# Row normalisation by the sum of magnitudes: eleven tiles of 12 and 8 rows against ten contiguous tiles of 13 and 12 rows

## The chip, the core and the metric

The kernel runs on one core of a Trainium2 chip. The metric is the time of one execution on the device, in microseconds; lower is better. The time before is the median of three runs.

## The reference

Each row of 1024 numbers is divided by the sum of its magnitudes.

```python
x = np.random.randn(32, 512, 1024).astype(np.float32)

def reference(x):
    sums = np.sum(np.abs(x), axis=-1, keepdims=True)
    return (x / (sums + 1e-8)).astype(np.float32)
```

Flattened, these are 16,384 rows of 4,096 bytes: 67.11 MB are read and 67.11 MB are written.

## The kernel before

The 16,384 rows are dealt to the 128 partitions of the on-chip memory, 128 rows to each. Work goes tile by tile; a tile holds so many rows in every partition. There are eleven tiles, numbered 0 to 10: ten of 12 rows and a last one of 8.

Where the rows lie in memory: the first 32 rows of every partition form a block called the head, in which a partition's rows are 32 x 4,096 = 131,072 bytes apart from the next partition's. Tiles 0 and 1 take rows 0 to 23 of the head, and tile 10 takes the last 8 rows of it. Tiles 2 to 9 are each one contiguous stretch of memory, in which partitions are 12 x 4,096 = 49,152 bytes apart.

Four buffers of 12 rows go round. `load(i)` (its transfer is issued at L86, on the queue of SyncE, SP) fills one; `store(i)` (issued at L91, on the queue of ScalarE, ACT) empties it; `load(i + 4)` can be issued only when the store of tile i has landed. The order is written out by hand: four loads, and then for each tile the computation, the store and the load of the tile four places on.

`max_dma_last_dim` sets the longest contiguous piece, here called a packet, that one descriptor of a transfer moves. A partition's share of a 12-row tile is 49,152 bytes; it goes as one packet (`WHOLE`) or as two of 24,576 (`HALF`). Loads of tiles 0 and 1 and stores of tiles 9 and 10 are whole; the other loads and stores go in halves. Stores of tiles 7 and 8 are issued as two transfers of 6 rows each.

`normalize` computes one tile: VectorE (DVE) sums the magnitudes of all rows in one instruction (L47), adds the epsilon (L54) and takes the reciprocal (L56), and multiplies the rows: the first ones in one instruction with the reciprocals broadcast (L58), some one by one (L65), and some on ScalarE (L68). The table `split` says how many rows go one by one on DVE and how many on ACT; tiles that it does not name are multiplied by L58 alone:

```python
split = {0: (3, 4), 1: (0, 3), 2: (0, 3), last - 1: (0, 2), last: (5, 3)}
```

Of the kernel before, what the change touches and what calls it, by code (L numbers as in the profile page):

```python
# [1 line left out]

# [4 lines left out]

FP32 = mybir.dt.float32
EPS = 1e-8


@with_exitstack
def kernel(
    ctx: ExitStack,
    tc: tile.TileContext,
    x: bass.AP,
    out: bass.AP,
):
    nc = tc.nc
    P = nc.NUM_PARTITIONS  # L20

    x_flat = x.flatten_outer_dims()
    out_flat = out.flatten_outer_dims()
    n, d = x_flat.shape

    R = 12
    BUFS = 4
    HEAD = 32
    per_partition = n // P
    assert n % P == 0 and (per_partition - HEAD) % R == 0  # L30
    rows = [R] * ((per_partition - HEAD) // R + 2) + [HEAD - 2 * R]

    def piece(flat, i):
        head = flat[: P * HEAD, :].rearrange("(p r) d -> p r d", p=P)
        if i < 2:
            return head[:, R * i : R * (i + 1), :]
        if i == len(rows) - 1:
            return head[:, 2 * R :, :]
        a = P * (HEAD + R * (i - 2))
        return flat[a : a + P * R, :].rearrange("(p r) d -> p r d", p=P)  # L40

    sbuf = ctx.enter_context(tc.tile_pool(name="sbuf", bufs=BUFS))
    stats = ctx.enter_context(tc.tile_pool(name="stats", bufs=len(rows)))

    def normalize(x_tile, k, kv, kt):
        s = stats.tile([P, R], FP32)
        nc.vector.tensor_reduce(  # L47
            out=s[:, :k],
            in_=x_tile[:, :k, :],
            axis=mybir.AxisListType.X,  # L50
            op=mybir.AluOpType.add,
            apply_absolute_value=True,
        )
        nc.vector.tensor_scalar_add(out=s[:, :k], in0=s[:, :k], scalar1=EPS)  # L54
        inv = stats.tile([P, R], FP32)
        nc.vector.reciprocal(out=inv[:, :k], in_=s[:, :k])  # L56
        if kv:
            nc.vector.tensor_mul(  # L58
                out=x_tile[:, :kv, :],
                in0=x_tile[:, :kv, :],  # L60
                in1=inv[:, :kv].unsqueeze(2).to_broadcast([P, kv, d]),
            )
        for r in range(kv, kv + kt):
            row = x_tile[:, r, :]
            nc.vector.tensor_scalar_mul(out=row, in0=row, scalar1=inv[:, r : r + 1])  # L65
        for r in range(kv + kt, k):
            row = x_tile[:, r, :]
            nc.scalar.activation(  # L68
                out=row,
                in_=row,  # L70
                func=mybir.ActivationFunctionType.Copy,
                scale=inv[:, r : r + 1],
            )

    last = len(rows) - 1
    split = {0: (3, 4), 1: (0, 3), 2: (0, 3), last - 1: (0, 2), last: (5, 3)}

    tiles = {}

    HALF, WHOLE = 24576, 49152

    def load(i):
        x_tile = tiles[i] = sbuf.tile([P, R, d], FP32, name="x_tile")
        nc.sync.dma_start(out=x_tile[:, : rows[i], :], in_=piece(x_flat, i), max_dma_last_dim=WHOLE if i < 2 else HALF)  # L86

    def store(i):
        parts = [(0, R // 2), (R // 2, R)] if i in (last - 3, last - 2) else [(0, rows[i])]
        for a, b in parts:  # L90
            nc.scalar.dma_start(  # L91
                out=piece(out_flat, i)[:, a:b, :],
                in_=tiles[i][:, a:b, :],
                max_dma_last_dim=WHOLE if i >= last - 1 else HALF,
            )

    def compute(i):
        k = rows[i]
        kt, ks = split.get(i, (0, 0))
        normalize(tiles[i], k, k - kt - ks, kt)  # L100

    with tc.manual_schedule():
        for i in range(BUFS):
            load(i)
        for i in range(len(rows)):
            compute(i)
            store(i)
            if i + BUFS < len(rows):
                load(i + BUFS)


# [1 line left out]
_INS = ['x']  # L113
_OUTS = [((32, 512, 1024), 'float32')]


# [23 lines left out]
```

## Time and profile before

| what | value |
|---|---|
| median of three runs | 316.8 us (316.76 to 316.91) |
| the profiled execution, whole time | 316.79 us |
| its span, first to last instruction | 315.2 us (315.16) |
| outside the span | 1.6 us |
| DVE busy | 261.1 us, 83% |
| ACT busy | 17.4 us, 6% |
| DMA packets, bytes | 5504, 134.22 MB |

The span is what the profiler shows between the first and the last instruction of the program. SPq and ACTq are the sequencers that issue transfers. "DMA share" is the mean busy share of the core's 16 DMA engines; a packet is put down to the stretch in which it starts, so that a short stretch can show more than 1.00.

### The profile page before, as it was taken

The page shows a single profiled execution, that of the slowest core. Times are in us where ns is not written, and L with a number is a line of the kernel's source. Part 1 is how long each engine was busy: PE and PEld are TensorE (multiplying, and loading weights), DVE is VectorE, ACT ScalarE, POOL GpSimd, SP SyncE. Part 2 cuts the span into 40 slices and gives each one's busy share as a digit, 9 for nine tenths or more (in the row PEclk, how much of TensorE's full clock was granted, in tenths as well). Part 3 has the DMA queues.
Part 4 walks back from the last instruction along what each step waited for, and adds up shares of the span by engine and source line. Part 5 has one row for each costly group of instructions (what it writes and reads, how often), then busy time and mean ns, then how long its engine had stood idle before and what let it go on. Part 6 is the DMA issues. An engine that isn't in the chain of part 4 may idle for free.

```text
span 315.2 us, 169 instructions
## 1 busy us (share of the span) xinstructions
DVE 261.1 (83%) x51; ACT 17.4 (6%) x16; POOL 0.2 (0%) x4
## 2 busy tenths in 40 slices
DVE  0079999999999999979996997999699969999100
ACT  0010403004000000000000000000000000203000
POOL 0000000000000000000000000000000000000000
DMA  7999999999999999999999999999999999999997
GB/s 299 499 399 409 440 399 418 430 449 418 430 449 418 430 449 424 424 449 427 421 449 427 421 449 434 415 449 434 415 449 434 415 433 449 416 433 499 399 403 329
DMA packets 5504, 134.22 MB, mean 426 GB/s; under 512 B 384, under 2 KB 384, under 8 KB 384
## 3 DMA queue, kind: packets, MB, share of 16 engines
q1 hardware_dynamic: 2736, 67.11, 49.9%
q10 hardware_dynamic: 2768, 67.11, 49.4%
HBM read 67.11 MB, written 67.11 MB: 426 GB/s over the span
## 4 chain that ended last, share of the span: by engine, by line
DVE 41%; DMA 33%; another core or an unknown queue 18%; SPq 0%; issue 0%; DVEq 0%
DVE s L47 23%; DMA x_tile<-in_x_dram 17%; DVE x_tile L58 15%; DMA out_dram<-x_tile 15%; DVE x_tile L65 2%; DVE inv L56 0%; DVE s L54 0%; SPq L86 0%; DVEq L135 0%
## 5 line engine op out<-in xcount | busy, mean ns | idle before, releaser
L47 DVE TENSOR_REDUCE s<-x_tile 128x12 f32<-128x12288 f32 (+1 forms) x11 | 138.2, 12561 | 30.0 <-DMA x_tile<-in_x_dram 30.0
L58 DVE TENSOR_TENSOR x_tile<-x_tile,inv 128x12288 f32<-128x12288 f32 (+3 forms) x10 | 113.6, 11358 | 0.5
L68 ACT ACTIVATE x_tile<-x_tile,inv 128x1024 f32<-128x1024 f32 x15 | 16.1, 1138 | 257.1 <-DVE inv L56 257.1
L65 DVE TENSOR_SCALAR x_tile<-x_tile,inv 128x1024 f32<-128x1024 f32 x8 | 5.5, 748 | 0.0
L56 DVE RECIPROCAL inv<-s 128x12 f32<-128x12 f32 (+1 forms) x11 | 2.5, 226 | 0.4
L68 ACT ACT_TABLE_LOAD x1 | 1.3, 1283 | 17.8 <-DMA x_tile<-in_x_dram 17.8
L54 DVE TENSOR_SCALAR s<-s 128x12 f32<-128x12 f32 (+1 forms) x11 | 1.9, 173 | 0.4
L124 POOL MEMSET const-uint8-127<- 128x1 uint8 x1 | 0.1, 102 | 0.0
L124 POOL MEMSET const-bfloat16-1.0<- 128x1 bf16 x1 | 0.1, 101 | 0.0
L124 POOL MEMSET const-float32-0.0<- 128x1 f32 x1 | 0.1, 98 | 0.2 <-issue 0.2
L124 POOL MEMSET const-float32-1.0<- 128x1 f32 x1 | 0.1, 98 | 0.0
## 6 DMA issues: line engine op xcount, KB each, us to landing
x_tile<-in_x_dram SPq DMA_DIRECT2D x10, 6144.0 KB, 37.6
out_dram<-x_tile ACTq DMA_DIRECT2D x8, 6144.0 KB, 47.2
out_dram<-x_tile ACTq DMA_DIRECT2D x4, 3072.0 KB, 36.5
x_tile<-in_x_dram SPq DMA_DIRECT2D x1, 4096.0 KB, 32.0
out_dram<-x_tile ACTq DMA_DIRECT2D x1, 4096.0 KB, 21.7
```

Of the source, the lines that this page charges most:

```text
L47: nc.vector.tensor_reduce(out=s[:, :k], in_=x_tile[:, :k, :], axis=mybir.AxisListType.X, op=mybir.AluOpType.add, apply_absolute_value=True,)
L54: nc.vector.tensor_scalar_add(out=s[:, :k], in0=s[:, :k], scalar1=EPS)
L56: nc.vector.reciprocal(out=inv[:, :k], in_=s[:, :k])
L58: nc.vector.tensor_mul(out=x_tile[:, :kv, :], in0=x_tile[:, :kv, :], in1=inv[:, :kv].unsqueeze(2).to_broadcast([P, kv, d]),)
L65: nc.vector.tensor_scalar_mul(out=row, in0=row, scalar1=inv[:, r : r + 1])
L68: nc.scalar.activation(out=row, in_=row, func=mybir.ActivationFunctionType.Copy, scale=inv[:, r : r + 1],)
L124: nc = _bacc.Bacc("TRN2", target_bir_lowering=False, num_devices=1)
```

## The change

The head is gone. The 128 rows of a partition are cut into ten tiles, 0 to 9, of 13, 13, 13, 12, 13, 13, 13, 12, 13 and 13 rows, each of them one contiguous stretch of memory. The four buffers have names of their own and hold 13, 13, 13 and 12 rows.

Packets: loads of tiles 0 and 1 move 53,248 bytes a packet; loads of tiles 2 to 6 go in half shares of 26,624 bytes (24,576 for tile 3). Loads of tiles 7, 8 and 9 are issued as two transfers, of the first 7 rows and of the rest, one packet a partition each. Stores of tiles 0 to 7 are one transfer each, in half shares; the store of tile 8 moves 53,248 bytes a packet. The last tile is summed, scaled and stored in two parts, of 7 rows and of 6; in each, three rows go to ACT and the rest one by one on DVE. `split` gives tile 0 five rows on ACT instead of four, and tile 8 three.

```diff
-    R = 12
-    BUFS = 4
-    HEAD = 32
...
-    rows = [R] * ((per_partition - HEAD) // R + 2) + [HEAD - 2 * R]
+    ROWS = [13, 13, 13, 12]
...
+    rows = []
+    while sum(rows) < per_partition:
+        rows.append(min(ROWS[len(rows) % len(ROWS)], per_partition - sum(rows)))
+    first = [sum(rows[:i]) for i in range(len(rows))]
+    last = len(rows) - 1
+    BUFS = len(ROWS)
+    WHOLE = 4 * d * max(ROWS)
+    UPPER = 7
 
-    def piece(flat, i):
-        head = flat[: P * HEAD, :].rearrange("(p r) d -> p r d", p=P)
-        if i < 2:
-            return head[:, R * i : R * (i + 1), :]
-        if i == len(rows) - 1:
-            return head[:, 2 * R :, :]
-        a = P * (HEAD + R * (i - 2))
-        return flat[a : a + P * R, :].rearrange("(p r) d -> p r d", p=P)
+    def piece(flat, i, a, b):
+        start = P * first[i]
+        return flat[start : start + P * rows[i], :].rearrange("(p r) d -> p r d", p=P)[:, a:b, :]
 
-    sbuf = ctx.enter_context(tc.tile_pool(name="sbuf", bufs=BUFS))
+    sbuf = ctx.enter_context(tc.tile_pool(name="sbuf", bufs=1))
...
-    def normalize(x_tile, k, kv, kt):
+    def normalize(x_tile, a, b, kt, ks):
+        k = b - a
...
-            in_=x_tile[:, :k, :],
+            in_=x_tile[:, a:b, :],
...
-    split = {0: (3, 4), 1: (0, 3), 2: (0, 3), last - 1: (0, 2), last: (5, 3)}
+    split = {0: (3, 5), 1: (0, 3), 2: (0, 3), last - 1: (0, 3)}
...
     def load(i):
-        x_tile = tiles[i] = sbuf.tile([P, R, d], FP32, name="x_tile")
-        nc.sync.dma_start(out=x_tile[:, : rows[i], :], in_=piece(x_flat, i), max_dma_last_dim=WHOLE if i < 2 else HALF)
+        k = rows[i]
+        x_tile = tiles[i] = sbuf.tile([P, ROWS[i % BUFS], d], FP32, name=f"x{i % BUFS}")
+        parts = [(0, UPPER), (UPPER, k)] if i >= last - 2 else [(0, k)]
+        for a, b in parts:
+            nc.sync.dma_start(
+                out=x_tile[:, a:b, :],
+                in_=piece(x_flat, i, a, b),
+                max_dma_last_dim=4 * d * k // 2 if i >= 2 and len(parts) == 1 else WHOLE,
+            )
 
-    def store(i):
-        parts = [(0, R // 2), (R // 2, R)] if i in (last - 3, last - 2) else [(0, rows[i])]
-        for a, b in parts:
-            nc.scalar.dma_start(
-                out=piece(out_flat, i)[:, a:b, :],
-                in_=tiles[i][:, a:b, :],
-                max_dma_last_dim=WHOLE if i >= last - 1 else HALF,
-            )
+    def store(i, a, b):
+        nc.scalar.dma_start(
+            out=piece(out_flat, i, a, b),
+            in_=tiles[i][:, a:b, :],
+            max_dma_last_dim=4 * d * rows[i] // 2 if i < last - 1 else WHOLE,
+        )
 
     with tc.manual_schedule():
         for i in range(BUFS):
             load(i)
-        for i in range(len(rows)):
-            compute(i)
-            store(i)
-            if i + BUFS < len(rows):
+        for i in range(last):
+            normalize(tiles[i], 0, rows[i], *split.get(i, (0, 0)))
+            store(i, 0, rows[i])
+            if i + BUFS <= last:
                 load(i + BUFS)
+        for a, b in ((0, UPPER), (UPPER, rows[last])):
+            normalize(tiles[last], a, b, b - a - 3, 3)
+            store(last, a, b)
```

More of the change, by code (lines that the diff above doesn't have):

```diff
@@ L24 @@
     n, d = x_flat.shape
-    R = 12
-    BUFS = 4
-    HEAD = 32
+    ROWS = [13, 13, 13, 12]
     per_partition = n // P
-    assert n % P == 0 and (per_partition - HEAD) % R == 0
-    rows = [R] * ((per_partition - HEAD) // R + 2) + [HEAD - 2 * R]
-    def piece(flat, i):
-        head = flat[: P * HEAD, :].rearrange("(p r) d -> p r d", p=P)
-        if i < 2:
-            return head[:, R * i : R * (i + 1), :]
-        if i == len(rows) - 1:
-            return head[:, 2 * R :, :]
-        a = P * (HEAD + R * (i - 2))
-        return flat[a : a + P * R, :].rearrange("(p r) d -> p r d", p=P)
-    sbuf = ctx.enter_context(tc.tile_pool(name="sbuf", bufs=BUFS))
-    stats = ctx.enter_context(tc.tile_pool(name="stats", bufs=len(rows)))
-    def normalize(x_tile, k, kv, kt):
-        s = stats.tile([P, R], FP32)
+    assert n % P == 0
+    rows = []
[10 more added lines that the diff above has]
+    sbuf = ctx.enter_context(tc.tile_pool(name="sbuf", bufs=1))
+    stats = ctx.enter_context(tc.tile_pool(name="stats", bufs=len(rows) + 1))
+    def normalize(x_tile, a, b, kt, ks):
+        k = b - a
+        s = stats.tile([P, max(ROWS)], FP32)
         nc.vector.tensor_reduce(
             out=s[:, :k],
-            in_=x_tile[:, :k, :],
+            in_=x_tile[:, a:b, :],
             axis=mybir.AxisListType.X,
@@ L54, in normalize @@
         nc.vector.tensor_scalar_add(out=s[:, :k], in0=s[:, :k], scalar1=EPS)
-        inv = stats.tile([P, R], FP32)
+        inv = stats.tile([P, max(ROWS)], FP32)
         nc.vector.reciprocal(out=inv[:, :k], in_=s[:, :k])
+        kv = k - kt - ks
         if kv:
             nc.vector.tensor_mul(
-                out=x_tile[:, :kv, :],
-                in0=x_tile[:, :kv, :],
+                out=x_tile[:, a : a + kv, :],
+                in0=x_tile[:, a : a + kv, :],
                 in1=inv[:, :kv].unsqueeze(2).to_broadcast([P, kv, d]),
@@ L63, in normalize @@
         for r in range(kv, kv + kt):
-            row = x_tile[:, r, :]
+            row = x_tile[:, a + r, :]
             nc.vector.tensor_scalar_mul(out=row, in0=row, scalar1=inv[:, r : r + 1])
         for r in range(kv + kt, k):
-            row = x_tile[:, r, :]
+            row = x_tile[:, a + r, :]
             nc.scalar.activation(
@@ L73, in normalize @@
             )
-    last = len(rows) - 1
-    split = {0: (3, 4), 1: (0, 3), 2: (0, 3), last - 1: (0, 2), last: (5, 3)}
+    split = {0: (3, 5), 1: (0, 3), 2: (0, 3), last - 1: (0, 3)}
     tiles = {}
-    HALF, WHOLE = 24576, 49152
     def load(i):
-        x_tile = tiles[i] = sbuf.tile([P, R, d], FP32, name="x_tile")
-        nc.sync.dma_start(out=x_tile[:, : rows[i], :], in_=piece(x_flat, i), max_dma_last_dim=WHOLE if i < 2 else HALF)
-    def store(i):
-        parts = [(0, R // 2), (R // 2, R)] if i in (last - 3, last - 2) else [(0, rows[i])]
+        k = rows[i]
+        x_tile = tiles[i] = sbuf.tile([P, ROWS[i % BUFS], d], FP32, name=f"x{i % BUFS}")
+        parts = [(0, UPPER), (UPPER, k)] if i >= last - 2 else [(0, k)]
         for a, b in parts:
-            nc.scalar.dma_start(
-                out=piece(out_flat, i)[:, a:b, :],
-                in_=tiles[i][:, a:b, :],
-                max_dma_last_dim=WHOLE if i >= last - 1 else HALF,
-            )
[L97 to L100, printed above, removed]
+            nc.sync.dma_start(
+                out=x_tile[:, a:b, :],
+                in_=piece(x_flat, i, a, b),
+                max_dma_last_dim=4 * d * k // 2 if i >= 2 and len(parts) == 1 else WHOLE,
+            )
+    def store(i, a, b):
[4 more added lines that the diff above has]
+        )
     with tc.manual_schedule():
```

## The prediction

> **What bounds the kernel now.** I read the page's first and third parts, then busy time by stretches, then the timeline of the end.
>
> ```profile
> span 315.2 us, 169 instructions
> DVE 261.1 (83%) x51; ACT 17.4 (6%) x16; POOL 0.2 (0%) x4
> DMA  7999999999999999999999999999999999999997
> q1 hardware_dynamic: 2736, 67.11, 49.9%
> q10 hardware_dynamic: 2768, 67.11, 49.4%
> ```
>
> Loads (q1) and stores (q10) together keep the 16 DMA engines busy for 99.3% of the span; DVE, the busiest compute engine, is idle for 54 us of it. The chain of waits names DVE for 41% and a 12-row sum as its largest member, which taken alone would point at DVE. The stretches, cut at the start of the first data packet and at the end of the last, decide between the two:
>
> ```profile
> 0.00:1.70 1.70, 0.00 (x0) 0.00 (x0) 0.20 (x4) 1.00 0.00 0
> 1.70:313.85 312.15, 261.12 (x51) 17.42 (x16) 0.00 (x0) 1.00 1.00 430
> 313.85:315.20 1.35, 0.00 (x0) 0.00 (x0) 0.00 (x0) 1.00 0.00 0
> ```
>
> The column before the last is the DMA share. Once the first packet starts no DMA engine is ever out of work: 1.00 over 312.15 us. So the time is 1.73 us of start, 312.12 us of packets back to back (1.73 to 313.85), 1.31 us of closing the program (to 315.16), and 1.63 us outside the span: 316.79 us, which is 0.01 under the median. The compute is wholly covered:
>
> ```profile
> 290.44 1.99 DVE x_tile L65 x3
> ```
>
> This last piece of the chain ends at 292.4 us, 21 us before the last packet; what follows is the draining of stores already issued.
>
> The trace's packet records, grouped by size, say what the 312.12 us consist of. A packet of 16,384 bytes takes 611 ns, 24,576 takes 912, 32,768 takes 1,213 and 49,152 takes 1,815; a 4-byte completion takes 9. That is a straight line: 301 ns for each 8,192 bytes (27.2 bytes a ns on each engine), and 8.7 ns for being a packet at all. Over 344 packets an engine the line gives 311.1 us. What remains is 0.82 us on each engine's first packet (2.49 to 2.76 us for 49,152 bytes) and again some 0.8 us at 40.5 to 43 us, where load packets are stretched just before the first store packet starts. Nothing else is lost.
>
> **The change part by part.** *Bytes.* 67.11 MB each way before and after; at the same 27.2 bytes a ns they cost the same.
>
> *Packets.* Before, 5,120 data packets and 16 x 24 transfers = 384 completions. After: loads 2 x 128 (tiles 0, 1), 5 x 256 (tiles 2 to 6), 3 x 256 (tiles 7 to 9, two transfers of one packet) = 2,304; stores 8 x 256, 128 and 2 x 128 = 2,432; together 4,736. Transfers are 13 loads and 11 stores, again 24. So 384 packets go, 24 on each engine, at 8.7 ns: **-0.21 us**. Sizes 20,480, 26,624 and 28,672 lie between measured ones; 53,248 lies beyond 49,152, where the line gives 1,966 ns. If that size had an extra price, 3 x 128 packets use it, 24 an engine; 10 ns on each, as much as another packet's own overhead, would be +0.24. I take 0 and keep 0 to +0.24.
>
> *Where partitions lie.* Tiles 0, 1 and 10 go from a pitch of 131,072 bytes to 53,248. In the records, 49,152-byte packets at the pitch of 131,072 (loads of tiles 0 and 1, but for the first) and at 49,152 (store of tile 9) both take 1,815 ns: 0. The Trainium skill ("DMA: Bandwidth & Descriptors", Latency and other measured facts) warns of memory pitches at large powers of two and states a drop from 214 to 207 GB/s at 512 KiB, the smallest it lists; if that 3% already held at 128 KiB, the 64 row moves of the old head would have lost about 2 us that the change returns, an estimate by that page, and the equal packet times speak against it.
>
> *The two starts.* The first packets' 0.82 us: kept, or grown with the packet (53,248/49,152), +0.07. The stretch at the first store: cause not shown by the trace. It could vanish (-0.8) or double (+0.8); the nearest row is itself, one first store before and one after, so 0.
>
> *Does any engine's queue run dry?* That needs both queues empty. One row moved one way costs 312.12 / 256 = 1.219 us. Sums grow by (12,950 - 8,679)/4 = 1,068 ns a row, L58 by (12,958 - 10,825)/2 = 1,067. Beginning: tile 0 lands 8 x (1.966 - 1.815) = 1.2 us later, at 18.9; the sum is 14.0, small steps 0.5, L58 5.5 and L65 2.1 (ACT's five rows, 5 x 1.14, are inside that), so its store issues at 41.0 instead of 38.75. The 51 rows in the first four loads last to 1.73 + 51 x 1.219 = 63.9. Cover: 23 us. Middle: a 13-row tile costs DMA 26 x 1.219 = 31.7 us and DVE 14.0 + 0.5 + 14.0 = 28.5; DVE keeps ahead by 3 us a tile. SP's loads still wait for the store four tiles back and the later loads stand behind them, but then the store queue is full. End: the last 6 rows are 7.3 us of DMA, so their store must be issued by about 306, and the first part's 8.5 us earlier, by 298. As a late bound, let tile 8 land when tile 9 lands now (255.7): DVE needs 14.0 + 0.5 + 10.8 for it, then 7.6 + 0.5 + 2.8 and 6.5 + 0.5 + 3.2 (ACT's three rows) for the two parts: 281, 292 and 302. From 222 of the 256 moves being done when the last load lands (34 rows loaded before the first store packet at 43.2, then 94 loads in turn with 94 stores), I estimate 273 for it, 268 for tile 8 done and 290 for the last issue: cover of 4 to 16 us. So DVE losing 7 rows of L58 (7.5 us), ACT's five more rows, and the last tile's extra four small DVE instructions net to 0 on the end. On ACT the first part's store, 0.34 us to issue, stands ahead of the second part's three rows; two more load issues of 0.37 us stand on SP. All inside that cover.
>
> *Splitting transfers.* Two more loads, two fewer stores; price by the 9 ns completion, none. The Trainium skill (same page, Anatomy of one DMA) puts about 2 us of fixed cost on every transfer; the count stays at 24, and by the records a completion takes 9 ns of an engine while the next transfer's packets follow at once, so here that cost is latency, not engine time.
>
> *Tail.* Engines end between 313.3 and 313.85 now; the slowest counts. The spread is carried from the start and may shift by 0.3 either way; closing 1.31 and outside 1.63 stay.
>
> Sum: 316.79 - 0.21 = **316.6 us**.
>
> **The rivals.** *Starting costs repeat (slower).* The 0.82 us at the first store could be the price of an engine beginning a transfer shaped unlike its neighbour's, and the three two-part loads bring three such meetings between about 180 and 273 us. Price 0.82 each: 316.6 + 3 x 0.82 = 319.0. One is not enough to count (317.4), two are (318.2). Against it: now 16,384-byte load packets meet 24,576-byte stores at 255 to 278 us and only four packets are stretched, by 0.12 us at most.
>
> *Both queues run dry at the end (slower).* If the second part's store issues after 306, every us later is one us more; 5 us of delay give 321.6. It needs DVE to be later than the latest case above.
>
> *The start gets cheaper (faster).* The old head sets the 16 engines' first reads and first stores at multiples of one large pitch; if the 0.8 us at the first store comes from that, it goes: 316.6 - 0.8 = 315.8. For it: the stretch appears exactly when a head tile's store joins. Against it: later head packets show none.
>
> *The split does nothing.* If the last tile's first sum waited for both parts, the order of work would be as with one part, at the same 316.6: the end has cover. The instruction lists show a separate wait for each part.
>
> **How the numbers follow.** A measurement of this kernel tells 0.2%, 0.63 us, from no change. Forecast, within that: 0.80. Repeated starts 0.09 and dry queues 0.03: slower 0.12. Cheaper start: faster 0.08. The forecast's own range is 316.58 - 0.3 (spread) to 316.58 + 0.07 + 0.24 + 0.3 and to 317.4 with one more start's price; it holds about 0.77. Downward it is stretched to the cheaper start at 315.8, which leaves out some 0.15.
>
> **What would show it.** Right: DMA share 1.00 from 1.73 to about 313.6, 5,120 packets, the four measured sizes unchanged, 53,248 bytes in about 1,966 ns, the last store issued near 290. Wrong: a stretch with DMA share under 1, packets of one size taking different times, or a last issue past 306.

## The result, and the profile after

The changed kernel takes 319.11 us (median of six, 318.77 to 320.05) against 316.74 us for the kernel before (median of six): 0.8% slower, ratio 1.0078 with a 95% interval of 1.0067 to 1.0089. The forecast was 316.6, within what a measurement tells from no change, with a range of 315.8 to 317.4; measured was 2.4 us more than before, outside that range. The spread of the six runs is 1.3 us where the kernel before has 0.3.

The page of the changed kernel:

```profile
span 316.8 us, 177 instructions
DVE 255.0 (80%) x52; ACT 22.7 (7%) x21; POOL 0.2 (0%) x4
DMA  8999999999999999999999999999999999999995
q1 hardware_dynamic: 2512, 67.11, 49.6%
q10 hardware_dynamic: 2608, 67.11, 49.2%
q14 instruction: 1, 0.01, 0.0%
```

Packets fell to 2,512 + 2,608 = 5,120 as counted, and DVE lost 6 us of work. Yet the span grew by 1.6 us, and the last digit of the DMA row fell from 7 to 5. The stretches, cut where the first and the last of the 16 DMA engines finish their last packet:

```profile
0.00:1.70 1.70, 0.00 (x0) 0.00 (x0) 0.20 (x4) 1.00 0.00 0
1.70:313.24 311.54, 254.99 (x52) 22.72 (x21) 0.00 (x0) 1.00 1.00 430
313.24:315.62 2.38, 0.00 (x0) 0.00 (x0) 0.00 (x0) 1.00 0.17 72
315.62:316.80 1.18, 0.00 (x0) 0.00 (x0) 0.00 (x0) 1.00 0.00 0
```

The engines are as full as before up to 313.24 us. Then for 2.38 us only some of them still work (share 0.17). Nothing ran dry: DVE and ACT were done in time, and the last store was issued at 291.9 us (290 forecast), as the timeline says:

```profile
291.88 0.34 ACTq L93 DMA_DIRECT2D out_dram<-x  x1
```

The packet records give the end of each engine's last packet. Before: first 313.33, median 313.54, last 313.85. After: first 313.25, median 313.61, last 315.62. So the typical engine finishes when it did, and six finish 0.4 to 2 us behind it; the kernel waits for the slowest. Of the profiled execution's 2.12 us (318.91 against 316.79), 1.77 are the last engine, -0.16 the closing of the program behind it, and 0.52 lie outside the span (2.15 us against 1.63).

Sizes keep the line of the prediction (26,624 bytes 987 ns, 28,672 bytes 1,062, 53,248 bytes 1,966), but some packets stand above it, which the prediction had named as a sign of being wrong. Besides those at the two starts, fourteen do between 205 and 260 us, by 0.06 to 0.67 us, 5.0 us in sum, all near the places where one load's packets end and the next one's begin (212, 230, 245, 257 to 259 us); eight of them are packets of the store that runs beside. The kernel before has three such packets after 50 us, 0.3 us in sum.

### The profile page after: what moved, and what is told of

It is laid out like the page before. It is cut to its first block, busy times and chain, and to the rows that moved or that the text cites. A ratio compares the mean times of both kernels' runs of the same rounds, so it can differ in the third digit from the quotient of the medians.

```text
span 316.8 us, 177 instructions
## 1 busy us (share of the span) xinstructions
DVE 255.0 (80%) x52; ACT 22.7 (7%) x21; POOL 0.2 (0%) x4
## 3 DMA queue, kind: packets, MB, share of 16 engines
q1 hardware_dynamic: 2512, 67.11, 49.6%
q10 hardware_dynamic: 2608, 67.11, 49.2%
## 4 chain that ended last, share of the span: by engine, by line
DVE 36%; DMA 35%; another core or an unknown queue 19%; ACT 1%; SPq 1%; issue 0%; ACTq 0%
DVE s L49 22%; DMA x<-in_x_dram 20%; DMA out_dram<-x 15%; DVE x L61 12%; DVE x L68 1%; ACT x L71 1%; SPq L86 1%; DVE inv L58 0%; DVE s L56 0%; ACTq L93 0%
## 5 line engine op out<-in xcount | busy, mean ns | idle before, releaser
L49 DVE TENSOR_REDUCE s<-x 128x13 f32<-128x13312 f32 (+3 forms) x11 | 138.2, 12563 | 34.4 <-DMA x<-in_x_dram 34.4
L61 DVE TENSOR_TENSOR x<-x,inv 128x10240 f32<-128x10240 f32 (+3 forms) x9 | 106.0, 11773 | 0.5
L71 ACT ACTIVATE x<-x,inv 128x1024 f32<-128x1024 f32 x20 | 21.4, 1137 | 249.7 <-DVE inv L58 249.7
L68 DVE TENSOR_SCALAR x<-x,inv 128x1024 f32<-128x1024 f32 x10 | 6.9, 748 | 0.1
L58 DVE RECIPROCAL inv<-s 128x13 f32<-128x13 f32 (+3 forms) x11 | 2.5, 230 | 0.4
L56 DVE TENSOR_SCALAR s<-s 128x13 f32<-128x13 f32 (+3 forms) x11 | 1.9, 174 | 0.4
```

What stands on the lines that cost most here:

```text
L49: nc.vector.tensor_reduce(out=s[:, :k], in_=x_tile[:, a:b, :], axis=mybir.AxisListType.X, op=mybir.AluOpType.add, apply_absolute_value=True,)
L61: nc.vector.tensor_mul(out=x_tile[:, a : a + kv, :], in0=x_tile[:, a : a + kv, :], in1=inv[:, :kv].unsqueeze(2).to_broadcast([P, kv, d]),)
L71: nc.scalar.activation(out=row, in_=row, func=mybir.ActivationFunctionType.Copy, scale=inv[:, r : r + 1],)
```

## The experiments

Three theories were set against each other first. *Layout*: tiles 0 and 1 no longer in the head start the engines apart. *Two-part loads*: tiles 7 to 9. *Last tile*: its second part. Every kernel was timed beside the kernel before (316.8 to 316.85 us each time), so the ratios compare. "First spread" is the time between the first and last of the 16 completions of tile 0's load, "last engine" the end of the last data packet, both from the packet records of one profiled execution. An engine's records form a chain, each starting 3 to 4 ns before the one ahead of it ends, so that one engine can mostly be followed from end to start.

**1. The kernel before, all tiles contiguous.**

```diff
     def piece(flat, i):
-        head = ...
+        start = P * sum(rows[:i])
+        return flat[start : start + P * rows[i], :].rearrange(...)
```

> The kernel before, with the head taken away: all eleven tiles contiguous, 12 rows each and 8 in the last; packets, transfers and order unchanged. Layout theory (the old head kept the 16 engines in step at the start, the contiguous layout lets them drift apart): 318 us or more, the 16 completions of the first load spread by 1 us instead of 0.39, the last engine ends over 1.5 us after the first. Two-part theory (the split loads of tiles 7 to 9 cost it) and last-tile theory: 316.7, spreads as before (0.4 at the first load, 0.5 at the end).

Measured: 317.65 us, ratio 1.0023 (1.0013 to 1.0033). First spread 1.21 us, engines end from 313.35 to 314.78. The layout alone costs 0.8 us, by spreading the engines: a third of the loss.

**2. The changed kernel, one transfer a load.**

```diff
-        parts = [(0, UPPER), (UPPER, k)] if i >= last - 2 else [(0, k)]
+        parts = [(0, k)]
```

> The changed kernel, with loads of tiles 7, 8 and 9 as one transfer each, in two half-share packets a partition. Two-part theory: most of the 2.4 us comes back, 317.2 or less, and no load or store packet over its line by more than 0.1 us after 50 us. Layout theory: 318.7 to 319.1, the last engine still 2 us behind the first at the end, with only the stretched packets at 211, 230, 245 and 258 us gone (some 0.4 us of the last engine).

Measured: 317.51 us, ratio 1.0019 (1.0011 to 1.0028): 1.6 us come back. After 50 us no packet stands above its line; the last engine ends at 314.14. Both theories hold a part. The edit takes two things along: 1.87 us lie outside the span instead of 2.15, and a program fetch among the last stores is gone (see numbers 7 to 10).

**3. The changed kernel, the last tile in one part.**

```diff
-        for a, b in ((0, UPPER), (UPPER, rows[last])):
-            normalize(tiles[last], a, b, b - a - 3, 3)
-            store(last, a, b)
+        normalize(tiles[last], 0, rows[last], rows[last] - 6, 6)
+        store(last, 0, rows[last])
```

> The changed kernel, with the last tile summed, scaled and stored in one part (7 rows on DVE one by one, 6 on ACT); its load still in two. Last-tile theory (the 2.4 us lie in the second part's store and what it adds at the end): 317 or less. Layout and two-part theories: 319.1, since the last issue at 292 us has 14 us of queued stores ahead of it in the changed kernel.

Measured: 318.9 us, ratio 1.0067 (1.0054 to 1.0080), as far from 317 as two of the theories said. But the number alone would mislead. Its timeline and stretches around 298 us:

```profile
277.71 14.02 DVE L49 TENSOR_REDUCE s<-x 128x13 f32<-128x13312 f32 x1 [7.17 <-DMA x<-in_x_dram]
...
298.63 0.35 ACTq L93 DMA_DIRECT2D out_dram<-x  x1
```
```profile
296.00:300.00 4.00, 0.98 (x2) 2.60 (x3) 0.00 (x0) 1.00 0.69 293
300.00:302.00 2.00, 0.00 (x0) 0.00 (x0) 0.00 (x0) 1.00 0.99 426
```

The store of 13 rows is issued at 298.6, when the store of tile 8 is all but drained, and the DMA share falls to 0.69. All 16 engines then end within 0.14 us, at 315.27 to 315.41. This is the prediction's dry-queue rival, called up by other means: it levels the engines and costs about as much as the late ones did. The two parts of the last tile are what keeps the changed kernel from running dry. The prediction's last rival took it that one part would do as well ("at the same 316.6: the end has cover"); it does not.

**4. The changed kernel with a head of 39 rows** for tiles 0, 1 and 9 (pitch 159,744 bytes).

```diff
+    HEAD = rows[0] + rows[1] + rows[last]
     def piece(flat, i, a, b):
+        if i in (0, 1, last):
+            ...  # rows of the head
```

> The changed kernel, with tiles 0, 1 and 9 in a head of 39 rows a partition (pitch 159,744 bytes) as the kernel before had them in one of 32; all else as changed. Layout theory: the 16 completions of the first load spread by 0.4 us again, and 317.3 or less. If only a pitch at a power of two keeps the engines in step: 319.1. Two-part and last-tile theories: 319.1.

Measured: 318.79 us, ratio 1.0055 (1.0042 to 1.0069), which overlaps the changed kernel's interval; first spread 1.36 us. This head does not bring the engines together. A single engine is late here (315.66 us, the next 314.15), with 1.5 us of stretched packets on it.

**5. The changed kernel, one transfer a load, one packet a partition.**

```diff
-        parts = [(0, UPPER), (UPPER, k)] if i >= last - 2 else [(0, k)]
+        parts = [(0, k)]
...
-                max_dma_last_dim=4 * d * k // 2 if i >= 2 and len(parts) == 1 else WHOLE,
+                max_dma_last_dim=4 * d * k // 2 if 2 <= i < last - 2 else WHOLE,
```

> The changed kernel, with loads of tiles 7 to 9 as one transfer each in whole-share packets (53,248 and 49,152 bytes). Count theory (two transfers to a tile cost the engines that lag): 317.5, as with one transfer in halves, no load or store packet over its line by 0.3 us between 205 and 260 us. Packet theory (one packet a partition beside half-share stores costs them): 318.5 or more, with such packets.

Measured: 319.67 us, ratio 1.0088 (1.0074 to 1.0102). But here another thing happens. Loads of 49,152- and 53,248-byte packets take 60 to 68% of the engines' time beside 26,624-byte stores; tile 7's load is in by 204.5 us, and tile 8's can be issued only at 205.9, when a store has landed. The load queue stands empty, and where it joins again, there and for tile 9 at 242 us, 87 packets are stretched, 23 us in sum, which is 1.45 us an engine. The third row is the changed kernel in the stretch of the second:

```profile
200.00:210.00 10.00, 10.00 (x1) 0.00 (x0) 0.00 (x0) 1.00 0.93 398
210.00:216.00 6.00, 6.00 (x2) 0.00 (x0) 0.00 (x0) 1.00 1.03 395
```
```profile
210.00:216.00 6.00, 3.35 (x1) 0.00 (x0) 0.00 (x0) 1.00 1.04 441
```

The second row is the one to read: the engines count as full (1.03) and move 395 GB/s, where the changed kernel moves 441 at a share of 1.04. Here a full DMA row does not prove a full rate.

**6. The changed kernel, parts in two packets a partition.**

```diff
-                max_dma_last_dim=4 * d * k // 2 if i >= 2 and len(parts) == 1 else WHOLE,
+                max_dma_last_dim=4 * d * (b - a) // 2 if i >= 2 else WHOLE,
```

> The changed kernel, with loads of tiles 7 to 9 in two transfers as changed, but two packets a partition in each (14,336, 12,288 and 10,240 bytes). Count theory: 319.1, late engines stretched where one part follows another. Packet theory: 317.5.

Measured: 318.32 us, ratio 1.0047 (1.0033 to 1.0061), between the two theories. All stretched packets between 205 and 290 us are gone, so these belong to the parts of one packet a partition; 0.8 us of the cost goes with them. The rest is not shown to be a cost of the count of transfers: in the profile the last engine (315.29) is one on which an 8,192-byte fetch of program falls at 303 us; it waits 0.3 us for it, and its next packet is 0.41 us longer. The next engine ends at 314.36, close to number 2.

**7 and 8. Two-part pieces put into the kernel before**: the last tile in two parts of 4 rows (7), and two-part loads of its last three tiles (8).

```diff
+        for a, b in ((0, 4), (4, rows[last])):
+            normalize(tiles[last], b - a, 0, b - a - 2, a)
+            nc.scalar.dma_start(...)
```

> The kernel before, with its last tile (8 rows) summed, scaled and stored in two parts of 4 rows, two rows of each on ACT; its load in one. Last-part theory (the longer program adds 0.4 us between the last data packet and the end of the measured time, as in the changed kernel against the version with one last part): 317.2, all of it behind the last packet. Without it: 316.8.

```diff
+        parts = [(0, (k + 2) // 2), ((k + 2) // 2, k)] if i >= last - 2 else [(0, k)]
+        for a, b in parts:
+            nc.sync.dma_start(...)
```

> The kernel before, with loads of tiles 8, 9 and 10 in two transfers (7 and 5, 7 and 5, 5 and 3 rows), one packet a partition in each. Two-part theory, if it acts by itself: 317.8 to 318.5, end spread of the engines 1.5 us or more. If it needs engines that already lag, as the contiguous start leaves them (1.4 us spread at the end there, 0.5 here): 316.8 to 317.2.

Measured: 317.26 us, ratio 1.0016 (1.0007 to 1.0025), and 317.49 us, ratio 1.0021 (1.0013 to 1.0030). For (8) the expected 1.5 us of end spread did not come (0.85 us), and only one of its load packets stands above its line after 50 us, by 0.17: where the engines are close together (first spread 0.45), one-packet parts cost little. Both kernels have one event in common with the changed kernel: an 8,192-byte fetch of program on one DMA engine at 296.5 us, among the last stores, with the store packet behind it 0.35 us longer. With the wait for the fetch that is 0.66 us on one engine, and in (7) and (8) this engine is the last (314.2 and 314.1); in the changed kernel it ends at 315.0, ahead of the last. The expectation for (7) put its cost behind the last packet; 0.36 us of it stand before that.

**9 and 10. The length of DVE's program.** The fetch falls into the drain (the time in which only stores are left) in all eight profiles with 66 or more DVE instructions, those of its sequencer included, and in none with 64 or fewer.

```diff
-            normalize(tiles[last], a, b, b - a - 3, 3)
+            normalize(tiles[last], a, b, 0, 3)
```

> The changed kernel, with DVE's rows of the last tile's two parts multiplied by one instruction a part instead of four and three: five DVE instructions fewer. Program theory (a DVE stream over 64 instructions brings one more fetch of an 8 KB piece of program, which delays the start by some tenths and lands on one DMA engine among the last stores): 318.2 to 318.7, 1.9 us outside the span instead of 2.15, the 8 KB fetch after the last data packet instead of at 297 us. Without it: 319.1.

```diff
+        step = 4 if x_tile is tiles.get(5) else R
+        for o in range(0, kv, step):
+            ...  # L58 on rows o to o + step
```

> The kernel before, with tile 5's L58 cut into three instructions of 4 rows: two more DVE instructions (66) in a stretch where DVE waits 2.6 us a tile for its load. Program theory: 317.2, with 1.77 us outside the span and an 8 KB fetch near 296 us, as in the kernel before with its last tile in two parts. Without it: 316.8.

Measured: 319.45 us for the shortened changed kernel, ratio 1.0080 (1.0068 to 1.0093): a miss. The fetch moved to 318.6 us, behind everything, as said, but other engines were late by then (last 315.71), and 2.58 us lay outside the span. The lengthened kernel before took 317.28 us, ratio 1.0013 (1.0004 to 1.0022), fetch at 296.5 us, as said. The engine that it strikes is the last there too (314.06, the next 313.81). So two more instructions can cost 0.5 us where the engines are together; that they cost the changed kernel anything was not confirmed.

**11. The changed kernel with a head of 32 rows** (pitch 131,072) for tiles 0, 1 and the last tile's second part.

```diff
+    HEAD = 32
     def piece(flat, i, a, b):
+        if i < 2 or (i == last and a == UPPER):
+            ...  # rows of the head
```

> The changed kernel, with a head of 32 rows a partition again (pitch 131,072 bytes) for tiles 0 and 1 and the last tile's second part; the other rows contiguous, tile 9's first part as a stretch of 7 rows a partition. Layout theory: the 16 completions of the first load spread by 0.4 to 0.6 us (0.9 to 1.4 in the runs without this pitch), 318.2 to 318.6; if the stretched packets at the two-part loads need engines that lag, those are gone too and it is 317.5 to 318.2. Without it: 319.1.

Measured: 317.96 us, ratio 1.0033 (1.0021 to 1.0046). 1.15 us come back, the two-part loads untouched. First spread 0.66 us, last engine 314.48; of the fourteen stretched packets four remain (2.1 us in sum). One of these is on the engine that ends last; the other three are on engines that without them would have ended at 313.2 to 313.5, ahead of the median (313.64). So such packets do not strike late engines alone.

**12. All three undone**: head of 32 rows; tiles 7 and 8 in one transfer, tile 9's two in half packets; one multiplying instruction a part.

> The changed kernel with all three undone: the head of 32 rows, loads of tiles 7 and 8 in one transfer and tile 9's two transfers in half packets, one multiplying instruction a part of the last tile. Ten tiles and 13-row buffers stay. If the three causes are all: 316.5 to 317.0, within 0.2% of the kernel before. If the 13-row tiles cost by themselves: 317.4 or more.

Measured: 317.33 us, ratio 1.0018 (1.0010 to 1.0027): above the range that three causes allowed, and close under what 13-row tiles were to cost. Its page settles which: the span is that of the kernel before.

```profile
span 315.2 us, 168 instructions
```

The last engine ends at 313.89. What is left, 0.5 us, lies outside the span (2.13 us against 1.63). The bytes begun after 313.0 us show the same repair; the rows are the kernel before, the changed kernel, experiment 11 and this one, the last column GB/s in the stretch:

```profile
313.00:313.90 0.90, 0.00 (x0) 0.00 (x0) 0.00 (x0) 1.00 0.01 0
```
```profile
313.00:313.90 0.90, 0.00 (x0) 0.00 (x0) 0.00 (x0) 1.00 0.39 164
```
```profile
313.00:313.90 0.90, 0.00 (x0) 0.00 (x0) 0.00 (x0) 1.00 0.20 82
```
```profile
313.00:313.90 0.90, 0.00 (x0) 0.00 (x0) 0.00 (x0) 1.00 0.01 0
```

**13 to 15. What lies outside the span: fewer ACT instructions** in the kernel before (13), in number 12 (14) and in the changed kernel (15).

```diff
-    split = {...}
+    split = {}
...
-            normalize(tiles[last], a, b, b - a - 3, 3)
+            normalize(tiles[last], a, b, 0, 3 if a else 0)   # (14) and (15)
```

> The kernel before, with all rows multiplied by L58 on DVE and none on ACT: 16 ACT instructions and 8 of DVE's fewer, same transfers. ACT-program theory (time outside the span goes with the number of ACT instructions): less than 1.6 us outside the span, 316.2 to 316.7. If the start of the program is as short as it gets at 50 ACT instructions: 316.8, nothing changed, since the last store still issues some 8 us before the stores run out.

> The version with all three causes undone (317.33 us, span as before, 2.13 us outside it), with ACT's rows given to DVE but for three in the last part: 17 ACT instructions fewer. ACT-program theory: 1.6 us outside the span, 316.6 to 316.9, even with the kernel before. Without it: 317.3.

> The changed kernel, with ACT's rows given to DVE but for three in the last part; loads, stores and layout as changed. ACT-program theory: 318.3 to 318.6, 0.5 us less than the changed kernel, all of it outside the span or behind the last packet; the last engine still over 2 us behind the first. Without it: 319.1.

Measured: 317.63, 318.27 and 320.39 us, ratios 1.0027 (1.0018 to 1.0036), 1.0045 (1.0033 to 1.0057) and 1.0111 (1.0090 to 1.0133). All three misses, and the theory falls: with 32 ACT instructions instead of 55, number 14 still has 2.20 us outside the span, and 13 has 1.81, more than the kernel before (1.63); only 15 has less than its kernel, 1.93 against 2.15. The kernels got slower inside the span. With DVE alone the store of tile 0 is issued at 44.1 us in (13) instead of 38.8 and at 47.7 in (14), and the next load, which waits for it, comes late: at 76.8 us in (13) and 81.9 in (14), in each when the load queue has been empty for over a us. Between 60 and 150 us, where the kernels that they come from have none, packets are stretched by 0.18, 0.35 and 0.67 us an engine. ACT's rows in the first tiles, hidden as they looked, set when the queues were refilled. That this is the whole loss is not shown: behind 200 us (15) has 0.57 us an engine against 0.34 in the changed kernel, on few engines, and its last four end at 316.0 to 317.9.

**16. Head of 32 rows and two packets a partition together** (11 with 6).

> The changed kernel with the head of 32 rows (317.96 us with it alone) and with two packets a partition in the parts of tiles 7 to 9 (318.32 us with that alone). If the two costs are apart: 317.2 to 317.4. If the stretched packets only strike engines that already lag: 317.7 to 318.0, as with the head alone.

Measured: 317.92 us, ratio 1.0032 (1.0021 to 1.0044): as with the head alone. Halving the packets adds nothing to the head. But the last engine is not late for the same reason: in number 11 it has 0.51 us of stretched packets, here none is stretched before 290 us, and the last engine (314.52, the next 314.10) is the one with the program fetch, 0.75 us on it. That the parts cost nothing once the engines start together is therefore not shown; the fetch may stand in for them.

**17. Can the joining cost be called up?** The kernel before, with loads of tiles 2 and 3 whole.

```diff
-max_dma_last_dim=WHOLE if i < 2 else HALF
+max_dma_last_dim=WHOLE if i < 4 else HALF
```

> The kernel before, with loads of tiles 2 and 3 in whole-share packets too. Beside half-share stores the loads then take two thirds of the engines, end near 69 us, and the load queue stands empty until the store of tile 0 has landed near 75 us. Joining theory (a queue that takes up again beside a running one stretches packets on every engine, as at the first store): stretched packets at 77 to 82 us, 0.5 to 1.4 us an engine, 317.3 to 318.2. Without it: no packet over its line between 50 and 150 us, 316.8.

Measured: 317.16 us, ratio 1.0005 (0.9996 to 1.0014). The load queue was empty from 73.2 us until the next issue at 77.2, and no packet is stretched there. Only the first store's start cost more beside whole packets (1.25 us an engine instead of 0.82). An empty queue by itself is not the cause; what else numbers 5, 13, 14 and 15 share stays open.

**18. The kernel before with a head of 36 rows** (tiles 0 to 2, pitch 147,456 bytes), all else contiguous.

> The kernel before, with a head of 36 rows a partition (pitch 147,456 bytes) for tiles 0, 1 and 2, and all other tiles contiguous, the last one too. If the pitch of 131,072 bytes is what keeps the first load's completions together: spread 0.9 us or more at the first load, 317.3 to 317.8, as with all tiles contiguous (317.65). If any long head does: spread 0.4 to 0.7 us, 316.8.

Measured: 316.87 us, ratio 1.0000 (0.9992 to 1.0009), first spread 0.63 us. Number 1 differs from it only in where tiles 0 to 2 lie, and takes 0.8 us more. The power of two is not needed.

## Why the prediction was wrong

**What held.** The bound, the bytes, the line of packet sizes and the 384 packets fewer. The sum of the packets does not close, though: 311.1 + 0.82 + 0.8 is 312.7, and 312.12 were to be explained. Consecutive records of an engine overlap by about 3 ns, 1.0 us over 344 packets, so a packet's own price is nearer 6 than 8.7 ns, and 24 fewer are worth 0.13 us instead of 0.21. That is too little to matter here. The engines never ran out of packets in the changed kernel; the last issue came at 292 for a forecast 290 and a deadline of 306, and the cover of DVE's and ACT's work was as worked out. The section that the prediction cites for a fixed cost of 2 us is on transfers issued by GpSimd; those here are issued by SP and ACT, and no run isolates such a cost.

**The step that failed first: "Where partitions lie ... 0".** It compared packet durations in the middle of a run, where they are equal at any pitch, and took that for the whole price. The price begins at the first load. In eleven profiles with tiles 0 and 1 at a pitch of 131,072 or 147,456 bytes the first spread is 0.39 to 0.69 us; in nine at 49,152, 53,248 or 159,744 bytes it is 0.76 to 1.36 us. Number 11 gives the size in the changed kernel (1.15 us), numbers 1 and 18 in the kernel before (0.8 us). Which property of the layout does it is open: 159,744 is a long pitch and does not help.

The rule that the prediction weighed there (the Trainium skill, "DMA: Bandwidth & Descriptors", Latency and other measured facts, pitches at large powers of two) lists no pitch under 512 KiB; carried down to 131,072 bytes it would have made leaving that pitch a gain. No run here shows such a loss at that pitch: number 18, at 147,456 bytes, takes the same time as the kernel before, and in the changed kernel going back to 131,072 gained 1.15 us.

**"Tail ... may shift by 0.3 either way; closing 1.31 and outside 1.63 stay."** This is the mis-sized term: the last engine came 1.77 us later, six times the allowance, and outside came 0.52 more. The prediction said that the slowest engine counts, and then kept the old spread with no row for it; what changed was the slowest, while the median moved by 0.07 us. A share of 1.00 over the whole stretch says that no engine had slack to catch up, so a late start is kept to the end; I read it only as a bound on what could be gained. Followed through the records, the last engine of the changed kernel is 0.4 to 0.7 us further behind at 60 us than the last engine of the kernel before, and gets 1.3 to 1.6 us of stretched packets between 205 and 260 us (before: 0.12). So on the engine that counts the two-part loads weigh more than the start.

**"Splitting transfers ... none."** This term was put at nothing from the price of a completion, which says nothing about the packets around it. Undoing the two-part loads brought back 1.6 us (number 2), making their packets half as large 0.8 (number 6, where the program fetch then decides). With two-part loads of one packet a partition, fourteen packets are stretched between 205 and 290 us in the changed kernel, four with the head of 32 rows (11), one in the kernel before (8), but also only three in number 4, whose engines start as far apart: the start bears on it, and how is not shown. Number 12, with both faults and DVE's longer program undone, has the span of the kernel before. The parts of this sum overlap, and so are not added up.

**The rivals.** "Starting costs repeat" named 319.0 us, and 319.11 was measured. It had the place right, the meetings of the two-part loads, but not the mechanism: 0.82 us on every engine at three places would be 39 us of stretched packets, and 5.0 were found, on some engines; the start that it left alone and the time outside the span made up the rest. The price was met by luck. "Both queues run dry" did not happen in the changed kernel, but did in number 3.

**Open.** The 0.5 us outside the span: 1.6 us in numbers 1, 3, 17, 18 and the kernel before, 2.1 to 2.2 in the changed kernel and numbers 4, 6, 11, 12, 14 and 16, 1.8 to 1.9 in numbers 2, 5, 7, 8, 10, 13 and 15, 2.6 in number 9. Neither fewer DVE instructions (9, 12) nor fewer ACT instructions (14) took it away; the last tile in one part (3) did, and why is not known. Also open is why one-packet parts stretch packets, and on which engines. No version beat the kernel before; number 18 equals it.

## What to carry to other kernels

In a kernel whose DMA engines are full from start to end, the time is that of the slowest engine: before you cost a change by bytes and packets, look at how far apart the engines' first and last packets end, and what in the change touches the first load. Here a change that was nearly free for the median engine cost the slowest 1.8 us. Compute that is hidden behind full queues still sets when the queues fill: moving ACT's hidden rows to DVE came with 0.8 to 1.3 us more (numbers 13 to 15).

## What the hardware showed that was not expected

Engines that start apart stay apart. In the changed kernel the first load's completions spread over 1.06 us (before: 0.39), and no packet is stretched between 60 and 205 us, so that no engine gains or loses there. The completions of later loads lie further apart, 1.94 to 2.02 us from tile 2's to the first part of tile 7's (before: 1.28), about one packet (0.99 us) more; as I read it, on some engines a packet of the store comes first. A DMA share of 1.00 or more can go with 395 GB/s instead of 430, when packets are stretched (number 5). With 66 or more DVE instructions an 8 KB fetch fell on one DMA engine in the drain in all eight profiles, and the store packet behind it took 0.35 to 0.45 us longer; with the wait, that engine lost 0.66 to 0.75 us, and in numbers 6, 7, 8, 10 and 16 it was the last to end.
